# Hybrid decoder step: the second recurrent block's inputs and scan are issued later, the decayed queries earlier, and one small output leaves by another queue

## The chip, the cores and the metric

One core of a Trainium2 chip. The metric is the device time of one execution in microseconds (us). The kernel before takes 1018.92 us, the median of three timed runs (1018.92, 1018.47 and 1023.57).

## The reference

One inference step of a one-layer decoder, on 560 tokens: 16 meta tokens, a prompt of 512, and 8 running sequences of 4 tokens each. All is float32.

```python
def trunk(x, W, states):
    x = x + 0.5 * swiglu(rmsnorm(x, g_ff1), ff1_gate, ff1_up, ff1_down)
    mix, new_st = mixer(rmsnorm(x, g_mix), W, states)
    x = x + mix
    x = x + 0.5 * swiglu(rmsnorm(x, g_ff2), ff2_gate, ff2_up, ff2_down)
    return rmsnorm(x, g_final), new_st
```

`mixer` has two halves that read the same normalised input. The first is a matrix-memory LSTM of four heads of 128: with queries q, keys k, values v and two gates per head it computes, chunk by chunk,

```python
s   = einsum('bhtd,bhsd->bhts', q, k) * w_intra
num = einsum('bhts,bhse->bhte', s, v) + w_inter * einsum('bhed,bhtd->bhte', C0, q)
den = sum(s, -1) + w_inter * einsum('bhd,bhtd->bht', n0, q)
h   = num / maximum(abs(den), exp(-m))
C   = decay * C0 + einsum('bhs,bhse,bhsd->bhed', w_state, v, k)
n   = decay * n0 + einsum('bhs,bhsd->bhd', w_state, k)
```

The second is a linear recurrence over 512 channels, held as four blocks of 128: a causal convolution of width 4 gives xc, two block-diagonal products give the gates r and i, and

```python
a    = exp(-8 * r * softplus(-lambda))
b_in = sqrt(1 - a*a) * (i * xc)
h[t] = a[t] * h[t-1] + b_in[t]
```

The outputs are the 544 rows of y and the new states of both halves.

## The kernel before

Everything is kept transposed: channels lie on the 128 partitions, tokens along the free axis. Each float32 weight tile is split into a high part (whi, cast on ACT, L259) and the rest (wlo, a subtraction on DVE, L264); a product is three matmuls for every tile and half of the tokens: whi by the high part of the input, whi by its low part, wlo by its high part (`split_mm`, L285; the products of the mixer have L296). Weights stream in on SP's queue (L226), six buffers deep. The two feed-forward networks take the time up to about 376 us and from about 645 us on; the mixer lies between.

In the mixer, PE makes 25 products of 1024 by 128: k, q, v, o for heads 0 to 3 and x, y for blocks 0 to 3. A step is one short function, named by a few letters and by its head or block. The table `PLAN` lists all steps in the order in which they are issued, and within `manual_schedule` this order is kept on PE, ACT, DVE and POOL alike, so that each engine works off its own instructions in that order and waits on semaphores for what other engines owe it. SP's DMAs alone are placed by the scheduler. The steps that matter here are these, for head h or block ct:

- `ev` (L1316, code L991) brings the product v from PSUM to the tile vT on DVE, multiplied by the norm's factor; `eq`, `ek`, `ex`, `ey`, `eo` do so for the other products.
- `cx` (L1165) is the convolution on DVE, `hx` (L1174) its split and two small copies on POOL (L1176, L1177), `a` and `b` the gate products on PE (L1191, prg).
- `cj` (L1226) makes the inputs of the recurrence on DVE, three instructions and a small memset (L1229 to L1232); `cd` (L1240) finishes them and runs the scan (L1243, L1244, L1246).
- `s` (L1433) makes the scores in PSUM (pA and pB), `m` (L1452) multiplies them on DVE into the weights W, `sd` (L1461) adds up the parts of W on POOL into D, `hd` (L1333) splits D into zh on ACT and zl on DVE (L1320, L1321).
- `qw` (L1471) makes on POOL the decayed queries qw (L1475) and their products qn with the normaliser state n0 (L1477), 128 by 32 each, and then adds a 32 by 32 piece of W to qn (L1479).
- `n` (L1482) makes numerator and denominator on PE. Its matmuls in order: two of four columns each on qw and the old state c0 (L1489), one on W and the values (L1493), two more on qw, and so on; the denominator takes zh after six of the columns' matmuls and zl near the end (L1497), and qn comes last (L1512). `cn` copies the result away on ACT.
- `cw` (L1565) decays c0 on POOL in eight pieces, `p` (L1554) makes px, what the new tokens add to the state, and `cp` (L1571) adds px to c0 on DVE (L1582) and sends it out.
- `cm` (L1528) splits the squares on ACT (L1531) and DVE (sql, L1532) and takes a maximum (dd, L1534); `f` (L1537) sums the squares on PE (pv, L1541); `cf` (L1544) adds that to dd on DVE (L1548) and takes the root. `vm` (L1378) makes Vm.

Products, scores, gates, n, p, f and the transposes all take turns in three PSUM buffers (tag "mm"); a product may start when the tile that was in its buffer three turns ago has been read. So n of head 1 takes the buffer of product v2, o1 takes that of px of head 2, and n of head 3 takes that of f of head 2. 23 buffers of 128 by 592 (`slot`) hold the tiles of the mixer.

The program's end (L849 to L885) finishes the last three output tiles, the norm, the output y and the last states. There SP and ACT both issue DMAs.

Of the kernel before, what the change touches and what calls it, by code (L numbers as in the profile page):

```python
# [8 lines left out]
ALU = mybir.AluOpType  # L9
# [27 lines left out]
k0 gc  # L37
q0 ek0 gd
k1 eq0 gf ge L0 ex0 cx0 tv0 gp ek1 hq0 hk0 gq hx0 gh
x1 am0 hk1 ex1 cv0  # L40
q1 a0 eq1 w0 b0 ta0 s0 m0 cx1 tk0 tb0 ck0 ca0
v1 sd0 ev1 hq1 L1 hx1 cb0 hd0 qw0 vm0 n0 cw0 a1 cc0 sk0 b1 cd0 cn0 ta1 cm0 tb1
k2 ca1 cb1 ek2 ci1 tv1 am1
x2 f0 cv1 p0 ex2 cf0 tk1 ck1 cp0 cj1 cx2
q2 L2 s1 w1 m1 sd1 eq2 hx2 hq2
v2 ev2 cd1 hd1 a2 ta2 ca2 b2 cb2 vm1 sk1 qw1 tb2 n1 cw1 cc2 cn1 hk2 am2 ce0
x3 cm1 ex3 f1 cf1 ce1
k3 w2 cl1 tv2 cx3
q3 cv2 ek3 hx3 eq3 p1 s2 tk2 cp1 cd2 ck2
v3 qw2 m2 vm2 L3 a3 sd2 hd2 ev3 n2 cw2 ta3 ca3 b3 hk3 cb3 cn2 tv3 tb3 cc3 sk2 am3 cd3  # L50
o0 p2 hq3 cv3 ce2 ce3 eo0 cl2 cl3 cm2 w3 cp2
y0 qw3 to0 ln lr ey0 gy0
o1 eo1 mo0 s3 my0 m3 f2 sd3
y1 tk3 hd3 cf2 to1 ey1 gy1 ck3 so0 mo1 n3 cw3 sk3 cn3 cm3
y2 ey2 so1 f3
# [18 lines left out]
LATER = 3  # L74
# [54 lines left out]
WO = (0, 512, 912, 1184, 1328, 1344)  # L129
# [5 lines left out]
O_HP, O_HS, O_CP, O_CS, O_NP, O_NS = 0, 4, 36, 48, 144, 148  # L135
# [4 lines left out]
def hymba_step(ctx, tc, xT, wgu1, wdn1, win, wout, wgu2, wdn2, consts, small, c0t, wrg,  # L140
               y, o_small, o_m, o_cp, o_cs):
    nc = tc.nc
    act, dve, pool, pe = nc.scalar, nc.vector, nc.gpsimd, nc.tensor
# [175 lines left out]
    osm = cst.tile([P, NOUT], F32, name="osm")  # L319
# [20 lines left out]
    def tmp(name="tmp"):  # L340
        return tp.tile([P, T], F32, tag="t", name=name)
# [8 lines left out]
    class Norm:  # L350
# [38 lines left out]
        def mean(self):  # L389
            self.ps = [aux_tile("psn")[:, :(T - self.c0) // 2] for _ in range(2)]  # L390
            for hf in range(2):
                pe.matmul(self.ps[hf], one_m[1024], self.acc[:, self.half(hf)], start=True, stop=True)
            self.t = tmp("rn")
# [263 lines left out]
    n1 = Norm(G1, 0)  # L657
# [90 lines left out]
    n2 = Norm(G2, C16)  # L748
    n2.open()
    spill = ctx.enter_context(tc.tile_pool(name="spill", bufs=1, space=bass.MemoryType.DRAM))  # L750
    kv = spill.tile([LATER, 2, P, 516], F32, name="kv")
    kv4 = spill.tile([LATER, C16, 257], F32, name="kv4")
    mixer(tc, dict(locals()))


    with tc.tile_pool(name="hp2", bufs=1) as hp, tc.tile_pool(name="sp2", bufs=1) as sp:
# [41 lines left out]
        h = ffn(1, n2, C16, hp, FF2, MID2, dict(ar=out_start, o=out_both, kr=reload, kt=reload4))  # L798
# [5 lines left out]
        def scale(a, b, eng, d0, d1, q):  # L804
            x = X[:, d0:d1, C16 + a:C16 + b]
            eng.tensor_tensor(x, x, rf[:, a:b].unsqueeze(1).to_broadcast([P, d1 - d0, b - a]), op=ALU.mult)
            q.dma_start(y[d0:d1, :, a:b].rearrange("d p t -> p d t"), x)

        def last_mm(hf, d, fs):
            a, b = parts[hf]  # L810
            for f in fs:
                wh, wl = w[d - TAIL][(f - c0) // 4]
                o = (f - c0) % 4 * P
                for m, (u, v) in enumerate(((wh, h[f][0]), (wh, h[f][1]), (wl, h[f][0]))):
                    pe.matmul(pd[d - TAIL][:, hf, :b - a], u[:, o:o + P], v[:, C16 + a:C16 + b],  # L815
                              start=f == c0 and m == 0, stop=f == c1 - 1 and m == 2)
# [3 lines left out]
        def into_x(hf, d):  # L820
            a, b = parts[hf]
            x = X[:, d, C16 + a:C16 + b]
            dve.scalar_tensor_tensor(x, pd[d - TAIL][:, hf, :b - a], 0.5, x, op0=ALU.mult, op1=ALU.add)
            sq[hf, d] = out_square(d, a, b)
# [7 lines left out]
        def root(hf):  # L832
            a, b = parts[hf]
            rsqrt(rf[:, a:b], sq[hf], tmp("rn")[:, :b - a])

        def state(i):
            (k, v), t = keys[i], tails[i]
            py = st[i] = mm_tile("st")[:, 0, :129]
            for j in range(4):
                pe.matmul(py, k[:, P * j:P * j + P], v[:, 129 * j:129 * j + 129], start=j == 0, stop=False)  # L840
            pe.matmul(py, t[:, :P], t[:, P:], start=False, stop=True)

        def state_out(i):
            act.copy(cp[:, i, :], st[i][:, :P])
            act.copy(osm[:, O_NP + i:O_NP + i + 1], st[i][:, P:])
            nc.scalar.dma_start(o_cp[i], cp[:, i, :])

        fs = range(c0, c1)
        with tc.manual_schedule(engines=MANUAL | {mybir.EngineType.Pool}):  # L849
            for d in range(TAIL, KD):  # L850
                last_mm(0, d, fs)
                into_x(0, d)
            a, b = parts[0]
            last_mm(1, TAIL, fs[:2])
            mean(0, 0)
            mean(0, 1)
            last_mm(1, TAIL, fs[2:4])
            mean(0, 2)
            last_mm(1, TAIL, fs[4:])
            root(0)  # L860
            scale(a, b, pool, 3, 4, nc.sync)
            scale(a, b, dve, 0, 3, nc.sync)
            into_x(1, TAIL)
            scale(a, b, dve, 4, 6, nc.sync)
            last_mm(1, TAIL + 1, fs)
            into_x(1, TAIL + 1)
            scale(a, b, dve, 6, 8, nc.sync)
            last_mm(1, TAIL + 2, fs)
            into_x(1, TAIL + 2)
            a, b = parts[1]  # L870
            for i in range(3):
                mean(1, i)
            root(1)
            st = {}
            cp = tmp("cp")[:, :LATER * P].rearrange("p (a b) -> p a b", b=P)
            for i in range(LATER):
                state(i)
            state_out(0)
            scale(a, b, pool, 7, 8, nc.scalar)
            state_out(1)  # L880
            scale(a, b, pool, 6, 7, nc.scalar)
            for d0, d1 in ((0, 1), (1, 3), (3, 5), (5, 6)):
                scale(a, b, dve, d0, d1, nc.sync)
            state_out(2)
            nc.sync.dma_start(o_small[:, O_NP:O_NP + LATER], osm[:, O_NP:O_NP + LATER])  # L885


@with_exitstack
def mixer(ctx, tc, e):
    nc = tc.nc  # L890
    act, dve, pool, pe = nc.scalar, nc.vector, nc.gpsimd, nc.tensor
    C, X, sm, om, osm, one_m = e["C"], e["X"], e["sm"], e["om"], e["osm"], e["one_m"]
    nm, n2 = e["nm"], e["n2"]
# [7 lines left out]
    def slot(name="slot", dtype=F32):  # L901
        return mp.tile([P, 592], dtype, tag="s", name=name, bufs=SLOTS)
# [7 lines left out]
    def blk4(ap):  # L910
        return ap.rearrange("p (b j) -> p b j", j=4)
# [392 lines left out]
    D = [{} for _ in range(H)]  # L1304
# [155 lines left out]
    @step  # L1460
    def do_sd(h):  # L1461
        W = D[h]["W"]
        S = D[h]["S"] = slot("D")
        pool.tensor_copy(S[:, 0:112], W[:, 0:112])
        pool.tensor_tensor(S[:, 112:512], W[:, 112:512], W[:, 512:912], op=ALU.add)
        pool.tensor_tensor(S[:, 240:512], S[:, 240:512], W[:, 912:1184], op=ALU.add)
        pool.tensor_tensor(S[:, 368:512], S[:, 368:512], W[:, 1184:1328], op=ALU.add)
        pool.tensor_tensor(S[:16, 496:512], S[:16, 496:512], W[:16, 1328:1344], op=ALU.add)

    @step  # L1470
    def do_qw(h):  # L1471
        d = D[h]
        qw = d["qw"] = mp.tile([P, NB, 4], F32, tag="qw", name="qw", bufs=2)
        qn = d["qn"] = mp.tile([P, NB, 4], F32, tag="qn", name="qn", bufs=2)
        pool.tensor_tensor(qw, blk4(d["q"][:, 512:TQ]), d["Wb"], op=ALU.mult)  # L1475
        n0 = d["n0"] = C[:, N0 + 8 * h:N0 + 8 * h + 8]
        pool.tensor_tensor(qn, qw, n0.unsqueeze(2).to_broadcast([P, NB, 4]), op=ALU.mult)  # L1477
        qs = qn.rearrange("p b j -> p (b j)")[:32]
        pool.tensor_tensor(qs, qs, d["W"][:32, WO[5]:WO[5] + 32], op=ALU.add)  # L1479

    @step
    def do_n(h):  # L1482
# [243 lines left out]
```

## Time and profile before

| | |
|---|---|
| timed runs | 1018.92, 1018.47, 1023.57 us |
| profiled execution, its own time | 1023.64 us |
| its span, first to last instruction | 1021.9 us |
| mean granted TensorE clock | 0.993 |
| busy: PE, DVE, ACT, POOL | 1013.1, 832.3, 559.5, 127.3 us |
| DMA | 102.85 MB, 101 GB/s |

The times of the rows below are microseconds from the first instruction. In a row of the timeline stand start, duration, engine, source line, operation, output and inputs, the number of instructions that were drawn together, and in brackets how long the engine had been idle and who ended it. In a row of the stage table stand the stretch and its length, then for PE, PE's weight loads, DVE, ACT and POOL the busy time (with the number of instructions), then the granted TensorE clock (1.00 is full speed), the DMA engines' busy share and GB/s.

### The profile page before, as it was taken

How to read it: one execution, taken by the hardware profiler on the slowest of the kernel's cores; microseconds unless marked ns; L12 is line 12 of the kernel's file. 1: busy time of each engine (PE TensorE's matmuls, PEld its weight loads, DVE VectorE, ACT ScalarE, POOL GpSimd, SP SyncE). 2: the span in 40 equal slices, each digit the busy share in tenths (PEclk: the TensorE clock that was granted, in tenths of full speed). 3: DMA queues.
4: the chain of work that ended last, by engine and by line, in shares of the span. 5: the costliest groups of instructions: out<-in, count | busy, mean ns of one | idle time of the engine just before them, and what ended most of it. 6: DMA issues, size and time to landing. Idle time of an engine off the chain costs nothing.

```text
span 1021.9 us, 20228 instructions
## 1 busy us (share of the span) xinstructions
PE 1013.1 (99%) x7778; PEld 997.5 (98%) x7778; DVE 832.3 (81%) x1480; ACT 559.5 (55%) x1074; POOL 127.3 (12%) x187
## 2 busy tenths in 40 slices
PE   9999999999999999999999999999999999999998
PEld 9999999999999999998999999999999999999997
DVE  7988888888788797889678765799888899859774
ACT  6544555565644464576666743554555665654543
POOL 1000000000000044382452202100000000000003
PEclk9999999999999999999799999999999999999999
DMA  6223233223332333325153133223323323335222
GB/s 234 92 79 103 89 100 104 94 95 103 89 104 68 106 116 130 102 81 146 35 133 103 57 104 108 73 64 103 112 87 102 105 94 114 93 102 156 81 70 96
DMA packets 61033, 102.85 MB, mean 101 GB/s; under 512 B 8560, under 2 KB 17024, under 8 KB 60936
## 3 DMA queue, kind: packets, MB, share of 16 engines
q1 hardware_dynamic: 60072, 101.11, 31.6%
q8 instruction: 61, 1.00, 0.4%
q10 hardware_dynamic: 864, 0.45, 0.2%
q14 instruction: 36, 0.29, 0.1%
HBM read 95.20 MB, written 6.33 MB: 99 GB/s over the span
## 4 chain that ended last, share of the span: by engine, by line
PE 88%; DVE 6%; ACT 2%; issue 1%; POOL 1%; DMA 1%; SPq 0%; DVEq 0%; POOLq 0%; ACTq 0%
PE pb L410 26%; PE pad L410 20%; PE pd L296 15%; PE po L296 7%; PE pu L296 4%; PE pg L296 3%; PE px L296 3%; PE pk L296 2%; PE py L296 1%; PE pq L296 1%; PE pn L1493 1%; DVE wlo L264 1%; PE pd L815 1%; PE pv L296 1%; PE pn L1489 1%
## 5 line engine op out<-in xcount | busy, mean ns | idle before, releaser
L259 ACT CAST whi<-raw 128x512 fp32r<-128x512 f32 (+2 forms) x289 | 172.3, 606 | 163.2 <-PE pad L410 41.3
L264 DVE TENSOR_TENSOR wlo<-raw,whi 128x512 fp32r<-128x512 f32 (+2 forms) x289 | 197.6, 700 | 65.5 <-ACT whi L259 62.7
L259 ACT CAST whi<-s 128x512 fp32r<-128x512 f32 x180 | 111.7, 621 | 105.2 <-PE pb L410 37.3
L264 DVE TENSOR_TENSOR wlo<-s,whi 128x512 fp32r<-128x512 f32 x180 | 124.1, 691 | 13.2 <-ACT whi L259 6.8
L410 PE MATMUL pad<-q21h,whi 128*128 128x280 f32 (+1 forms) x360 | 104.2, 290 | 0.1
L410 PE MATMUL pb<-qt4l,whi 128*128 128x280 f32 (+1 forms) x360 | 104.0, 289 | 0.0
L410 PE MATMUL pad<-q21l,whi 128*128 128x280 f32 (+1 forms) x360 | 104.0, 289 | 0.0
L410 PE MATMUL pad<-q21h,wlo 128*128 128x280 f32 (+1 forms) x360 | 104.0, 289 | 0.0
L410 PE MATMUL pb<-qt4h,whi 128*128 128x280 f32 (+1 forms) x360 | 103.9, 289 | 0.0
L410 PE MATMUL pb<-qt4h,wlo 128*128 128x280 f32 (+1 forms) x360 | 103.9, 289 | 0.0
L410 PEld LDWEIGHTS pad<-q21h,whi 128*128 128x128 f32 x360 | 67.8, 188 | 0.4 <-DVE z L429 0.4
L410 PEld LDWEIGHTS pb<-qt4h,whi 128*128 128x128 f32 x360 | 67.9, 189 | 0.0
L410 PEld LDWEIGHTS pb<-qt4h,wlo 128*128 128x128 f32 x360 | 67.8, 188 | 0.0
L410 PEld LDWEIGHTS pad<-q21l,whi 128*128 128x128 f32 x360 | 67.8, 188 | 0.0
L410 PEld LDWEIGHTS pb<-qt4l,whi 128*128 128x128 f32 x360 | 67.8, 188 | 0.0
L410 PEld LDWEIGHTS pad<-q21h,wlo 128*128 128x128 f32 x360 | 67.8, 188 | 0.0
L239 DVE TENSOR_TENSOR s<-raw 128x512 f32<-128x512 f32 x90 | 61.4, 682 | 2.0 <-DMA raw<-in_wdn 2.0
L296 PE MATMUL pd<-hl,whi 128*128 128x280 f32 (+1 forms) x294 | 61.6, 290 | 0.0
L296 PE MATMUL pd<-hh,whi 128*128 128x280 f32 (+1 forms) x294 | 61.4, 290 | 0.0
L296 PE MATMUL pd<-hh,wlo 128*128 128x280 f32 (+1 forms) x294 | 61.2, 289 | 0.0
L379 POOL TENSOR_TENSOR acc<-acc,sq 128x560 f32<-128x560 f32 (+1 forms) x6 | 9.1, 1518 | 405.3 <-ACT sq L378 405.3
L410 PE MATMUL pb<-q11h,whi 128*128 128x280 f32 (+1 forms) x180 | 52.4, 291 | 0.0
(470 smaller groups left out, 3008.0 us busy)
## 6 DMA issues: line engine op xcount, KB each, us to landing
raw<-in_wgu SPq DMA_DIRECT2D x174, 256.0 KB, 2.7
raw<-in_wdn SPq DMA_DIRECT2D x71, 256.0 KB, 2.7
raw<-in_win SPq DMA_DIRECT2D x50, 256.0 KB, 2.9
raw<-in_wout SPq DMA_DIRECT2D x16, 256.0 KB, 2.7
raw<-in_wdn SPq DMA_DIRECT2D x18, 192.0 KB, 2.4
c<-in_c0t SPq DMA_DIRECT2D x4, 512.0 KB, 5.4
out_o_cs<-c SPq DMA_DIRECT2D x4, 512.0 KB, 4.3
X<-in_xT SPq DMA_DIRECT2D x7, 280.0 KB, 5.4
```

The lines of the kernel that those rows point to most:

```text
L239: dve.tensor_tensor(q[k], q[x], q[y], op=op)
L259: act.copy(ready[i][0][:, :src.shape[-1]], src)
L264: dve.tensor_tensor(lo, src, hi, op=ALU.subtract)
L296: state["mm"] = pe.matmul(ps[:, hf, :n], a[:, ws], b[k][:, c0 + hf * n:c0 + hf * n + n], start=first and j == 0 and i == 0, stop=last and ...
L379: (dve if d == KD - 1 else pool).tensor_tensor(self.acc[:, c0:], self.acc[:, c0:], s[:, c0:], op=ALU.add)
L410: pe.matmul(ps, a[:, k * P:k * P + P], b, start=first and k == 0 and i == 0, stop=k == KD // 2 - 1 and i == 2, skip_group_check=not first)
L815: pe.matmul(pd[d - TAIL][:, hf, :b - a], u[:, o:o + P], v[:, C16 + a:C16 + b], start=f == c0 and m == 0, stop=f == c1 - 1 and m == 2)
L1489: pe.matmul(pn[:, 1, 4 * b:4 * b + 4], d["c0"][:, b, :], d["qw"][:, b, :], start=b == 0, stop=False)
L1493: pe.matmul(pn[:, 0, a:512], V[:KROWS[i], i, :P], W[:KROWS[i], WO[i]:WO[i] + 512 - a], start=i == 0, stop=i == 4)
```

## The change

Four things, three of them in the table and one at the end.

1. `cj1` (inputs of block 1's recurrence) leaves its place ahead of `cx2` and now stands, with `cd1` (scan of block 1), behind `ev2` and `hd1`. `hd1` thus comes ahead of both.
2. Each `qw` goes to where its head's `am` (the masked gates) ends, one to two rows up in the table. As its last instruction read W, which is not there yet at that place, that addition goes to the end of `sd`.
3. `cp2` comes ahead of `cm2` and `w3` instead of behind them.
4. The last DMA of the program, three columns of the normaliser states, is issued by ACT instead of SP.

The instructions are the same as before, apart from their places.

```diff
-x1 am0 hk1 ex1 cv0
+x1 am0 qw0 hk1 ex1 cv0
 q1 a0 eq1 w0 b0 ta0 s0 m0 cx1 tk0 tb0 ck0 ca0
-v1 sd0 ev1 hq1 L1 hx1 cb0 hd0 qw0 vm0 n0 cw0 a1 cc0 sk0 b1 cd0 cn0 ta1 cm0 tb1
-k2 ca1 cb1 ek2 ci1 tv1 am1
-x2 f0 cv1 p0 ex2 cf0 tk1 ck1 cp0 cj1 cx2
+v1 sd0 ev1 hq1 L1 hx1 cb0 hd0 vm0 n0 cw0 a1 cc0 sk0 b1 cd0 cn0 ta1 cm0 tb1
+k2 ca1 cb1 ek2 ci1 tv1 am1 qw1
+x2 f0 cv1 p0 ex2 cf0 tk1 ck1 cp0 cx2
 q2 L2 s1 w1 m1 sd1 eq2 hx2 hq2
-v2 ev2 cd1 hd1 a2 ta2 ca2 b2 cb2 vm1 sk1 qw1 tb2 n1 cw1 cc2 cn1 hk2 am2 ce0
+v2 ev2 hd1 cj1 cd1 a2 ta2 ca2 b2 cb2 vm1 sk1 tb2 n1 cw1 cc2 cn1 hk2 am2 qw2 ce0
 x3 cm1 ex3 f1 cf1 ce1
...
-v3 qw2 m2 vm2 L3 a3 sd2 hd2 ev3 n2 cw2 ta3 ca3 b3 hk3 cb3 cn2 tv3 tb3 cc3 sk2 am3 cd3
-o0 p2 hq3 cv3 ce2 ce3 eo0 cl2 cl3 cm2 w3 cp2
-y0 qw3 to0 ln lr ey0 gy0
+v3 m2 vm2 L3 a3 sd2 hd2 ev3 n2 cw2 ta3 ca3 b3 hk3 cb3 cn2 tv3 tb3 cc3 sk2 am3 qw3 cd3
+o0 p2 hq3 cv3 ce2 ce3 eo0 cl2 cl3 cp2 cm2 w3
+y0 to0 ln lr ey0 gy0
...
-            nc.sync.dma_start(o_small[:, O_NP:O_NP + LATER], osm[:, O_NP:O_NP + LATER])
+            nc.scalar.dma_start(o_small[:, O_NP:O_NP + LATER], osm[:, O_NP:O_NP + LATER])
...
     def do_sd(h):
...
+        qs = D[h]["qn"].rearrange("p b j -> p (b j)")[:32]
+        pool.tensor_tensor(qs, qs, W[:32, WO[5]:WO[5] + 32], op=ALU.add)
...
     def do_qw(h):
...
-        qs = qn.rearrange("p b j -> p (b j)")[:32]
-        pool.tensor_tensor(qs, qs, d["W"][:32, WO[5]:WO[5] + 32], op=ALU.add)
```

On DVE, around the evacuation of v2 (vT) and ahead of Vm of head 1, th and a_6071 are the inputs of block 1's recurrence, hs its scan, and zl<-D is the split of head 1:

```order
 L991 TENSOR_TENSOR vT<-pv,r 128x560
+L1321 TENSOR_TENSOR zl<-D,zh 128x512
+L1229 TENSOR_TENSOR th<-th,a_6071 128x584
+L1230 SCALAR_TENSOR_TENSOR th<-th,xc 128x584
+L1231 TENSOR_SCALAR a_6071<-a_6071 128x584
+L1232 MEMSET a_6071 128x8
 L1243 SCALAR_TENSOR_TENSOR th<-th 128x584
 L1244 COPY th<-C 128x8
 L1246 SCALAR_TENSOR_TENSOR hs<-a_6071,th 128x584
-L1321 TENSOR_TENSOR zl<-D,zh 128x512
 L1381 TENSOR_TENSOR Vm<-V5s,seqm 96x1024
```

The four instructions of `cj1` come from ahead of `cx2`, and the split now stands first behind vT; from Vm on the order is as it was.

On POOL, between the sums D of head 1 and the decay of its state c0 (c_5909 and c_5914 are the same tile), osm<-xp are the two copies of `hx2`:

```order
 L1467 TENSOR_TENSOR D<-D,W 128x144
 L1468 TENSOR_TENSOR D<-D,W 16x16
+L1470 TENSOR_TENSOR qn<-qn,W 32x32
 L1176 COPY osm<-xp 128x3
 L1177 COPY osm<-xp 128x24
-L1475 TENSOR_TENSOR qw<-qT,Wb 128x32
-L1477 TENSOR_TENSOR qn<-qw,C 128x32
-L1479 TENSOR_TENSOR qn<-qn,W 32x32
-L1568 TENSOR_SCALAR c_5909<-c_5909,Wb 128x128 x8
+L1568 TENSOR_SCALAR c_5914<-c_5914,Wb 128x128 x8
```

The decayed queries are gone from this place; they now stand ten instructions earlier, behind the masked gates of head 1, and only the addition of W is left.

On DVE, near the end of the product y0, c_6283 is the state of head 2, sql and dd are `cm2`, and rlt belongs to the recurrence's norm:

```order
 L991 TENSOR_TENSOR og<-po,r 128x544
 L1259 TENSOR_TENSOR lacc<-lacc,lsq 128x544 x2
+L1582 TENSOR_TENSOR c_6283<-c_6283,px 128x1024
 L1532 TENSOR_TENSOR sql<-sq,sqh 128x544
 L1534 TENSOR_TENSOR dd<-dd,Eb 128x544
-L1582 TENSOR_TENSOR c_6283<-c_6283,px 128x1024
 L264 TENSOR_TENSOR wlo<-raw,whi 128x512 x2
 L331 SCALAR_TENSOR_TENSOR rlt<-pl,rl 128x544
```

The addition that reads px of head 2 out of its PSUM buffer has moved ahead of two instructions, and what follows is unchanged.

## Prediction

> **What bounds the kernel now.** I read the page's engine row and its clock row first.
>
> ```profile
> PE 1013.1 (99%) x7778; PEld 997.5 (98%) x7778; DVE 832.3 (81%) x1480; ACT 559.5 (55%) x1074; POOL 127.3 (12%) x187
> PEclk9999999999999999999799999999999999999999
> ```
>
> PE is busy for 99% of the span, so only two things can be taken from it: idle time, and time at less than the full clock. The clock row is full but for one of forty slices, at half of the span, inside the mixer. Next come PE's waits, summed, number, longest:
>
> ```profile
> PE pn L1489 <- POOL qn L1477: 1.5, 1, 1.5
> PE po L296 <- DVE c L1582: 0.9, 1, 0.9
> ```
>
> The first is n of head 1, waiting for the decayed queries; the second is o1, waiting for `cp2`. The change moves what ends each of them. Then the table by stages: n of head 0, product x2 with f0, a stretch of DVE, the idle time, n of head 1, x3 with f1, the second idle time, the start of o1, and n of head 3.
>
> ```profile
> 443.68:449.35 5.67, 5.67 (x33) 4.18 (x33) 5.57 (x8) 1.32 (x3) 5.45 (x5) 1.00 0.62 192
> 457.90:464.13 6.23, 6.23 (x51) 6.23 (x50) 5.04 (x11) 4.75 (x10) 1.82 (x6) 1.00 0.40 123
> 470.97:492.99 22.02, 20.51 (x115) 17.09 (x113) 21.49 (x36) 12.49 (x24) 14.52 (x18) 0.81 0.46 134
> 482.20:483.71 1.51, 0.00 (x1) 0.03 (x1) 1.51 (x4) 1.27 (x2) 1.39 (x5) 1.00 0.16 37
> 483.71:493.84 10.13, 10.13 (x33) 7.33 (x34) 8.93 (x14) 5.64 (x6) 10.09 (x10) 0.54 0.21 73
> 493.84:502.24 8.40, 8.40 (x50) 8.40 (x51) 3.40 (x8) 4.63 (x11) 2.31 (x10) 0.74 0.18 62
> 547.30:548.21 0.91, 0.00 (x1) 0.00 (x1) 0.91 (x2) 0.89 (x2) 0.48 (x2) 1.00 0.00 0
> 551.00:555.00 4.00, 4.00 (x31) 3.90 (x31) 3.33 (x6) 2.33 (x5) 0.00 (x0) 1.00 0.39 137
> 564.18:570.13 5.95, 5.95 (x33) 4.45 (x34) 3.73 (x5) 5.27 (x9) 5.46 (x8) 1.00 0.00 1
> ```
>
> Right behind the idle 1.51 us the clock falls: 0.54 over n of head 1, 0.74 over x3. The same 33 matmuls take 10.13 us there and 5.67 at head 0, and x3 with f1 takes 8.40 where x2 with f0 takes 6.23. So the one wait costs 1.51 + 4.46 + 2.17 = 8.14 us. The idle 0.91 us at o1 was followed by no fall (1.00).
>
> The Trainium skill, page "TensorE: Matmul & The Clock Gate", section "Why this matters for your kernels", asks only for no idle gaps above about 3 us. The trace disagrees, with 1.51 us ahead of a half clock; by that rule the wait would cost 1.51 alone.
>
> **The wait at n of head 1.** PE, POOL and DVE around it, and two rows of head 0's time:
>
> ```profile
> 483.71 0.58 PE L1489 MATMUL pn<-qw,c 128*128 128x4 f32 x4 [1.51 <-POOL qn L1477]
> 481.86 0.54 POOL L1468 TENSOR_TENSOR D<-D,W 16x16 f32<-16x16 f32 x1
> 482.36 0.64 POOL L1176 COPY osm<-xp 128x3 f32<-128x3 f32 x1
> 483.11 0.24 POOL L1475 TENSOR_TENSOR qw<-qT,Wb 128x32 f32<-128x32 f32 x1
> 483.43 0.24 POOL L1477 TENSOR_TENSOR qn<-qw,C 128x32 f32<-128x32 f32 x1
> 470.97 0.76 DVE L1229 TENSOR_TENSOR th<-th,a 128x584 f32<-128x584 f32 x1
> 472.83 0.57 DVE L1169 TENSOR_SCALAR xc<-xp,C 128x584 f32<-128x584 f32 x1
> 482.88 0.73 DVE L991 TENSOR_TENSOR vT<-pv,r 128x560 f32<-128x560 f32 x1
> 486.62 1.21 DVE L1381 TENSOR_TENSOR Vm<-V5s,seqm 96x1024 fp32r<-96x1024 f32 x1
> 435.94 0.87 PE pB L1443 x6
> 444.12 0.49 SPq L1342 DMA_DIRECT2D Ab<-rows  x1
> ```
>
> The queries stand on POOL behind the D sums and two copies; moved up, they are done long before. What can still hold PE is vT, since n takes the PSUM buffer of product v2. `cj1` takes DVE from 470.97 to 472.83, 1.86 us. Without it there, the chain of convolution, weight split, scores' product and D sums runs 1.86 us earlier: vT ends at 482.88 + 0.73 - 1.86 = 481.75, ahead of the gate products' end at 482.20, and D at 481.86 + 0.54 - 1.86 = 480.54, so that its split is there before n wants it. I take this wait at nothing, with 0.45 us of cover; if vT were later than that, PE would wait for the excess. With no idle time, the clock should hold: -8.14 us on PE up to the end of x3. One wait is new ahead of this: as the `slot` buffers fall to other tiles, SP's load of head 1's gate rows (Ab) also waits for the scores of head 0 on PE, and later weights queue behind it on SP. It was issued at 444.12 and the scores end at 436.81, so it costs nothing.
>
> **What DVE gives back at f1.** The four instructions go back in behind vT, still ahead of Vm. DVE therefore does the same work before Vm, and Vm starts where it did, at 486.62. The stretch 470.97 to 492.99 above is 21.49 of 22.02 busy: DVE is full there, and the half clock hid it. Behind that stretch stand these rows:
>
> ```profile
> 496.22 0.69 DVE L1321 TENSOR_TENSOR zl<-kT,zh 128x512 fp32r<-128x512 f32 x1 [3.23 <-ACT zh L1320]
> 496.83 1.28 DVE L264 TENSOR_TENSOR wlo<-raw,whi 128x512 fp32r<-128x512 f32 x2
> 500.04 0.73 DVE L1532 TENSOR_TENSOR sql<-sq,sqh 128x544 fp32r<-128x544 f32 x1 [1.93 <-ACT sqh L1531]
> 500.68 0.72 DVE L1534 TENSOR_TENSOR dd<-dd,Eb 128x544 f32<-128x544 f32 x1
> 501.33 0.17 DVE L1158 COPY xp<-C 128x24 f32<-128x24 f32 x1
> 502.20 0.45 DVE L1160 TENSOR_TENSOR xp<-px,r 128x280 f32<-128x280 f32 x1 [0.70 <-PE px L296]
> 502.99 0.71 DVE L1548 TENSOR_TENSOR dd<-pv,dd 128x544 f32<-128x544 f32 x1
> 502.00 0.29 PE L1541 MATMUL pv<-sqh,ones_r 128*128 128x272 f32 x1
> ```
>
> The 3.23 and 1.93 us of idling wait for PE's late n and x3, and go. From 492.99 on, zl (0.61, start to start), two wlo (1.28 less 0.07 of overlap, as at zl) and sql (0.64) end at 495.45. PE's second matmul of f1 needs sql, and would be there at 502.00 - 8.14 + 0.13 (6.23 over 48) = 493.99. So PE waits 1.46 us at f1 and leaves it 6.68 us earlier than before, not 8.14. DVE then needs `cm1`'s maximum (0.65), a small fill (0.17) and the evacuation of x3 (502.99 - 502.20 = 0.79) ahead of L1548, which starts at 497.06 instead of 502.99: the vector chain is 5.93 us earlier. From below, were DVE 1.5 us quicker, f1 would not wait; from above, DVE's idle 0.53 us shows that a little more than 22.02 us is not excluded either. I take 1.46.
>
> **o1 and n of head 3.** Up to o1 PE has no other wait; DVE's rows there and at n of head 3:
>
> ```profile
> 545.67 0.71 DVE L1532 TENSOR_TENSOR sql<-sq,sqh 128x544 fp32r<-128x544 f32 x1
> 546.94 1.21 DVE L1582 TENSOR_TENSOR c<-c,px 128x1024 f32<-128x1024 f32 x1
> 563.41 0.71 DVE L1548 TENSOR_TENSOR dd<-pv,dd 128x544 f32<-128x544 f32 x1
> 563.79 0.27 PE L1356 MATMUL pt<-ident,t 128*96 128x128 f32 x1
> 564.18 0.61 PE L1489 MATMUL pn<-qw,c 128*128 128x4 f32 x4
> ```
>
> `cp2` now takes the place of sql: its addition ends at 545.67 - 5.93 + 1.21 = 540.95, and PE is ready at 547.30 - 6.68 = 540.62. A wait of 0.33 us is left and o1 starts 7.26 us earlier. But sql and dd follow it, so DVE as a whole is no earlier than its 5.93. At n of head 3 PE needs L1548 of `cf2`, which ends at 564.12; PE itself ended its transposes at 564.06, so there is no slack. With the change PE comes at 564.06 - 7.26 = 556.80 and the tile is free at 564.12 - 5.93 = 558.19: a wait of 1.39 us. What `cp2` won at o1 is given back there. n of head 3 starts 5.93 us earlier, and behind it no wait of PE's list is left but the end's.
>
> The other queries moved on POOL (heads 0, 2, 3) pass transposes' inputs and sums that PE takes later, and cost two times 0.24 us in front of them; POOL is 12% busy, and I put them at nothing. The same holds for the small copy of `cp2` on ACT, now ahead of the cast in `cm2`.
>
> **The end.**
>
> ```profile
> 1018.04 0.34 ACTq L846 DMA_DIRECT2D out_o_cp<-cp  x1
> 1018.80 0.46 SPq L885 DMA_DIRECT2D out_o_small<-osm  x1
> SPq L1707 <- DMA out_o_small<-osm: 1.5, 1, 1.5
> ```
>
> The last DMA is issued at 1018.80 behind SP's outputs, and the end waits 1.5 us for it. From ACT it can go behind the issue at 1018.04, at about 1018.40, 0.4 us sooner; then SP's last output, issued just ahead of it, is next. Between 0 and 0.46 us, I take 0.3.
>
> **The sum.** The profiled execution took 1023.64 us, its span 1021.9 and 1.7 around it: 1023.64 - 8.14 (idle and half clock) + 1.46 (f1) - 0.91 + 0.33 (o1) + 1.39 (n of head 3), which is -5.87 and agrees with DVE's 5.93, and - 0.3 at the end: 1017.5. How does that stand to the median? Two of the timed runs took 1018.47 and 1018.92, one 1023.57. The two lie 4.7 to 5.2 us below the profiled one, and a run in which the 1.51 us of idling did not bring the half clock would by this working take 1023.64 - 5.93 = 1017.7, because DVE's full stretch holds it all the same. So I read the median as a run without the half clock. There the change gains only what DVE lets it: the end's 0.3, 1018.4. Between 1017.5 and 1018.4 I forecast **1018.0 us**, no change that can be told: 0.5% or 5.1 us is about what a measurement of this kernel can tell from none.
>
> **Rivals.**
>
> *n of head 3 loses its clock.* Its wait of 1.39 us lies between the 0.91 that did nothing and the 1.51 that brought the half clock, and ahead of the same sparse matmuls. If the clock falls there, 4.46 + 2.17 = 6.63 us are lost and nothing behind recovers them, PE being full to the end: 1018.0 + 6.6 = 1024.6, slower. It decides from an idle time of somewhere between 0.91 and 1.51 us, and in the median only if most runs show it. For it: half of the four executions shown seem to have had it with 1.51. Against: 0.12 us less, and any slip of DVE's 5.93 shortens it. Chance 0.17. The same page of the Trainium skill, section "What's actually happening", has the clock judged in a free-running window of about 3.4 us; by that this would strike some runs and not others, and no run here shows the window.
>
> *DVE is no bound.* If DVE runs through its stretch quicker, PE keeps all: 1023.64 - 8.14 - 0.91 - 0.3 = 1014.3, at most 0.5% below the median. Against it stand 21.49 busy of 22.02. Chance 0.08, and this is the most that the rows allow.
>
> *The wait stays under another name.* If vT comes over 1.5 us later than worked out, PE idles for DVE instead of POOL, the clock falls, and the time is that of the profiled run less the end, 1023.3. Against: DVE's order is free of anything slow there. Chance 0.06.
>
> **The numbers.** My case has 0.69. Range 1015.2 to 1024.2: below, DVE half as much of a bound; above, the third case and most of the first rival. Faster by over 0.5% (below 1013.8) lies beyond even the second rival: 0.04. Slower by over 0.5% (above 1024.0) is most of the first rival: 0.13. Within: 0.83.
>
> **What would show it.** Right: no idle time at n of head 1, granted clock 1.00 from 480 to 505, new waits of PE for DVE's sql at f1 (about 1.5 us) and for L1548 at n of head 3 (about 1.4), o1's wait at about 0.3, and the last DMA issued on ACT near 0.4 us after ACT's last state. Wrong: a clock below 0.9 behind n of head 3, a wait for vT at n of head 1, or neither of the two new waits, which would mean that DVE was not full.

## The result and the profile after

The changed kernel took 1026.82 us (median of 8 executions, 1021.03 to 1027.14), the kernel before 1019.07 (8, 1018.45 to 1023.57). The ratio is 1.0052, interval 1.0031 to 1.0073: slower, where I had forecast 1018.0 and no change that can be told. The medians alone would give 1.0076. Neither median is that of one time: both kernels' executions fall into groups, and the mean granted clock goes with the groups.

| kernel | full clock | in between | lost most |
|---|---|---|---|
| before, 104 executions of all comparisons | 55 at 1018.2 to 1019.9 (clock 0.998 to 1.000) | 21 at 1021.5 to 1022.4 (0.994) | 28 at 1023.1 to 1024.6 (0.992 to 0.993) |
| changed, 19 executions | 4 at 1020.2 to 1021.0 (0.999 to 1.000) | 3 at 1022.0 to 1025.2 (0.993 to 0.998) | 12 at 1026.6 to 1027.2 (0.992 to 0.993) |

(Five executions of all kernels, with a mean clock below 0.9, are left out of these counts and those below.) A mean clock of 0.998 can hide one short stretch at half clock: 3.4 us at half lower the mean over 1020 us by 0.0017, and a profile with 0.998 told below has such a stretch. Of the 55, 11 have 0.998, all from 1019.2 us on; the group is counted as full clock all the same. So two things are to be explained: 1.9 us more at full clock (middle of the groups, 1018.75 and 1020.6), and about 6 us more in most executions.

The profiled execution of the changed kernel is one of the four: 1021.03 us, span 1019.3. Its engine row and its clock row:

```profile
PE 1007.0 (99%) x7778; PEld 991.6 (97%) x7778; DVE 835.3 (82%) x1480; ACT 559.7 (55%) x1074; POOL 129.8 (13%) x187
PEclk9999999999999999999999999999999999999999
```

Its waits of PE (sum, number, longest):

```profile
PE pv L1541 <- DVE sql L1532: 1.6, 1, 1.6
PE pn L1489 <- DVE dd L1548: 1.3, 1, 1.3
PE pt L1356 <- POOL t L1351: 1.2, 2, 0.8
...
PE pA L1443 <- DVE kT L993: 0.8, 1, 0.8
```

The wait for the queries and the half clock behind it are gone, and that for `cp2` at o1 too. The two new waits that were forecast are there with nearly the forecast sizes: 1.57 us at f1 (1.46) and 1.28 at n of head 3 (1.39). Two more were not forecast, for POOL's copy t and for DVE's kT; the one for kT stands in the kernel before as well, in an execution at full clock (0.82 us). The same in the rows of PE's timeline:

```profile
482.27 0.30 PE L1191 MATMUL prg<-xch,wrgl 128*128 128x292 f32 x1
482.41 0.50 PE L1489 MATMUL pn<-qw,c 128*128 128x4 f32 x4
...
494.35 0.29 PE L1541 MATMUL pv<-sqh,ones_r 128*128 128x272 f32 x1
496.21 0.39 PE L1541 MATMUL pv<-sql,ones_r 128*128 128x272 f32 x1 [1.57 <-DVE sql L1532]
...
561.54 0.61 PE L1489 MATMUL pn<-qw,c 128*128 128x4 f32 x4 [1.28 <-DVE dd L1548]
```

A before at full clock was needed to compare with. The profiled execution of the run "before, gap filled" below is one: it has the order of before and lost no clock. In this table stands where PE starts a step, in us behind its first matmul of product v1 in the same execution (timeline rows of the two runs and of four others told below):

| first matmul of | n head 1 | f1 | product k3 | scores head 2 | o1 | n head 3 | gate product, next network |
|---|---|---|---|---|---|---|---|
| before, full clock | 46.49 | 58.52 | 59.08 | 73.88 | 106.01 | 121.98 | 202.75 |
| changed, full clock | 44.76 | 56.70 | 59.04 | 73.88 | 105.60 | 123.89 | 204.66 |
| part 1 alone | 44.81 | 56.77 | 59.07 | 73.89 | 106.07 | 122.05 | 202.76 |
| part 2 alone | 46.43 | 58.48 | 59.09 | 73.90 | 106.49 | 122.45 | 203.23 |
| part 3 alone | 46.47 | 58.48 | 59.04 | 73.87 | 104.72 | 123.32 | 205.70 |
| changed, cp2 and last DMA as before | 44.76 | 56.70 | 59.02 | 73.86 | 106.48 | 122.46 | 203.07 |

PE reaches n of head 1 and f1 1.8 us sooner, waits, and starts k3 at the very place where it did. All that part 1 wins is given back there. At n of head 3 the changed kernel is 1.9 us later, and it keeps that to the end.

Where the 1.9 us come from is seen on ACT. First before, then the changed kernel, at gy0 (the Gelu of block 0):

```profile
549.83 1.28 ACT L1283 ACT_TABLE_LOAD   x1
552.75 0.66 ACT L1283 ACTIVATE yg<-yg 128x544 f32<-128x544 f32 x1 [1.64 <-DVE yg L991]
```

```profile
548.85 1.28 ACT L1283 ACT_TABLE_LOAD   x1 [3.05 <-DVE yg L991]
550.14 0.66 ACT L1283 ACTIVATE yg<-yg 128x544 f32<-128x544 f32 x1
...
550.71 1.65 ACT L259 CAST whi<-raw 128x512 fp32r<-128x512 f32 x3
```

Before, ACT loads the table of Gelu while it waits for yg. In the changed kernel the load stands behind that wait, and 1.28 us come on top of it. The trace shows what changed: at 548.8 us, right ahead of the load, stands a separate semaphore instruction of L1283, and before there is none ahead of that load. So the wait for DVE's yg is no longer carried by the activation but by an instruction of its own, and the load comes behind it. The reason as I read it in the programs, which no trace shows: with `cp2` ahead of `cm2`, the activation on yg must also wait for ACT's own sqh (L1531), and carries that wait instead. Behind it on ACT come weight casts, and behind those on DVE their rests, W, the split of D, and L1548 that n of head 3 waits for.

At the end, the last DMA was issued 0.43 us after ACT's last state, as forecast (0.4), and gave nothing:

```profile
1015.43 0.34 ACTq L846 DMA_DIRECT2D out_o_cp<-cp  x1
1015.86 0.41 ACTq L885 DMA_DIRECT2D out_o_small<-osm  x1
```

```profile
SPq L1707 <- DMA out_o_small<-osm: 2.1, 1, 2.1
```

From the issue of the last state to the end of the span it is 1019.3 - 1015.43 = 3.87 us; before, 1021.9 - 1018.04 = 3.86. From the issue of the small DMA to the end it is now 1019.3 - 1015.86 = 3.44 us instead of 1021.9 - 1018.80 = 3.10, so what the issue won is lost again behind it. The profile puts SP's last wait down to the small DMA. As the end stands equally far behind the last state in both, it may as well be that state's landing that SP waits for; no run here tells the two apart.

### The profile page after: what moved, and what is told of

Same layout as the page of the kernel before. It is cut to its first block, busy times and chain, and to the rows that moved or that the text cites. A ratio compares the mean times of both kernels' runs of the same rounds, so it can differ in the third digit from the quotient of the medians.

```text
span 1019.3 us, 20230 instructions
## 1 busy us (share of the span) xinstructions
PE 1007.0 (99%) x7778; PEld 991.6 (97%) x7778; DVE 835.3 (82%) x1480; ACT 559.7 (55%) x1074; POOL 129.8 (13%) x187
## 4 chain that ended last, share of the span: by engine, by line
PE 86%; DVE 7%; ACT 2%; issue 2%; DMA 1%; POOL 1%; SPq 1%; DVEq 0%; POOLq 0%; ACTq 0%
PE pb L410 27%; PE pad L410 20%; PE pd L296 15%; PE po L296 6%; PE pu L296 4%; PE pg L296 3%; PE px L296 2%; PE pk L296 2%; PE pq L296 1%; DVE wlo L264 1%; PE py L296 1%; PE pd L815 1%; PE pv L296 1%; ACT W L1423 1%; PE pn L1493 1%
## 5 line engine op out<-in xcount | busy, mean ns | idle before, releaser
L767 POOL TENSOR_TENSOR acc<-acc,sq 128x272 f32<-128x272 f32 (+2 forms) x10 | 9.6, 971 | 343.4 <-ACT sq L765 343.2
```

Of the source, the lines that this page charges most:

```text
L767: pool.tensor_tensor(acc[:, a:b], acc[:, a:b], s, op=ALU.add)
```

## The experiments

### Where the clock is lost

Theory A: the idle time ahead of n of head 3 brings a half clock. Theory B: the longer one at f1 does. The changed kernel once more, with no edit:

> The changed kernel once more, to see at which place the granted clock falls in its executions near 1026.8 us. Theory A (n of head 3): the idle 1.3 us ahead of n of head 3 brings the half clock, so a profiled execution near 1026.8 shows the clock at 0.5 behind about 561 us and full between 480 and 505. Theory B (f1): the idle 1.6 us ahead of f1's second matmul brings it, and the clock is at 0.5 behind about 496 us. Both expect a median of 1026.8 and a few executions near 1021.0.

Measured 1026.7 us median, ratio 1.0037 (1.0016 to 1.0059). The profiled execution was again one with a full clock (1020.19), so it could not show the place. Then the two gaps were filled, one each:

```diff
-        pv = ps["f", h] = mm_tile("pv")
+        pv = ps["f", h] = mm_tile("pv"); [pe.matmul(pv[:, 0, :272], ones_r[128], D[h]["sq"][0][:, :272], start=True, stop=True) for _ in range(10 if h == 1 else 0)]
```

> The changed kernel with ten more matmuls of 272 columns on PE ahead of f1 (they repeat f1's first one and are overwritten), so that PE is idle there for about 0.3 us instead of 1.57; the sums are the same, only work is added. Theory B (f1 brings the half clock): nearly all executions near 1021.0, mean clock 0.999. Theory A (n of head 3): median stays at 1026.8, clock 0.992. Both: in an execution with a full clock the time is 1021.0, since PE waits there for DVE anyway.

```diff
-        for i in range(4):
+        for i in [0, 1, 2, 3] * (4 if what == "k" and h == 3 else 1):
```

> The changed kernel with the four transposes of head 3's keys made four times over (the same values into the same place), so that PE is busy for about 1.3 us more ahead of n of head 3, whose wait falls from 1.3 us to below 0.4. Theory A (n of head 3 brings the half clock): nearly all executions near 1021.0, clock 0.999. Theory B (f1): median stays at 1026.8, clock 0.992.

With n of head 3 filled, all 12 executions lie between 1020.1 and 1020.8. With f1 filled, 8 lie at 1020.0 to 1020.6, one at 1021.65 and 3 at 1026.2 to 1026.7. Waits of PE with n of head 3 filled:

```profile
PE pv L1541 <- DVE sql L1532: 1.5, 1, 1.5
...
PE pn L1489 <- DVE dd L1548: 0.6, 1, 0.6
```

So f1's 1.5 us, left as they were, cost no clock in any of 12, and the wait at n of head 3 is needed for the loss: A. That filling f1 also made the loss rarer (3 of 12 at the full loss, against 12 of 19; 4 of 12 against 15 of 19 with the smaller losses) is not explained by A. These numbers do not settle whether it is chance.

Next, the wait at n of head 3 made longer:

```diff
+        [dve.tensor_tensor(nt, dd, dd, op=ALU.add) for _ in range(2 if h == 2 else 0)]
         dve.tensor_tensor(halves(dd, 272), pv[:, :, :272], halves(dd, 272), op=ALU.add)
```

> The changed kernel with two more additions on DVE (128 by 544, 0.72 us each, into a tile that is overwritten) ahead of the one that n of head 3 waits for, so that its idle time is about 2.7 us instead of 1.3. Theory A: every execution shows the half clock there, median 1020.5 + 1.4 + 6.3 = 1028.2, none below 1026. If the chance does not depend on the length of the idle time: a quarter of the executions at 1022.

Median 1028.86 us, all six between 1026.8 and 1030.0 with a clock of 0.991 to 0.993; A holds. Here the profile shows the place, in the row of PE's timeline and in the stages around it (granted clock is the third number from the right):

```profile
562.85 1.02 PE L1489 MATMUL pn<-qw,c 128*128 128x4 f32 x4 [2.87 <-DVE dd L1548]
```

```profile
494.00:500.00 6.00, 4.49 (x35) 4.27 (x34) 4.88 (x10) 1.04 (x1) 5.64 (x17) 1.00 0.26 90
...
560.00:566.00 6.00, 3.15 (x9) 2.12 (x9) 5.04 (x8) 4.29 (x5) 1.98 (x2) 0.73 0.10 36
566.00:572.00 6.00, 6.00 (x21) 4.48 (x20) 3.96 (x7) 2.72 (x6) 5.13 (x6) 0.50 0.00 0
572.00:578.00 6.00, 6.00 (x26) 5.50 (x26) 1.52 (x3) 2.96 (x7) 0.00 (x0) 0.50 0.00 0
578.00:585.00 7.00, 7.00 (x51) 7.00 (x51) 3.33 (x6) 1.79 (x3) 0.00 (x0) 0.87 0.23 77
```

Behind f1's wait (494 to 500) the clock stays at 1.00, behind n of head 3 it is half for 2 x (0.27 x 6 + 0.50 x 6 + 0.50 x 6 + 0.13 x 7) = 17.1 us.

The same on the kernel before, at n of head 1:

```diff
-        for hf in range(2):
+        for hf in [0] * (ct == 2 and g == 1) + [0, 1]:
```

> The kernel before with half of the last gate product ahead of n of head 1 (six matmuls) made twice, the same values into the same place, so that PE idles about 0.7 us there instead of 1.51. Theory A (an idle of 1.3 to 1.5 us ahead of n's sparse matmuls brings the half clock in a part of the executions): no execution near 1021.7 to 1023.8 any more, all between 1018.2 and 1020, median 1018.8, clock 0.998 to 1.000. If the half clock comes from elsewhere: about two in five executions stay above 1021.5.

A miss in size, by my own edit: half of a gate product is three matmuls, not six, so the idle time only fell to 1.16 us. Of 12 executions 8 lay at 1018.4 to 1019.6 and 4 at 1022.0 to 1022.5; the group near 1023.5 was gone. So 1.16 us there seem still too many for the clock to be safe; the place of these four losses was not profiled.

### Which part costs what

Each part alone on the kernel before, as numbered under the change. Part 1:

```diff
-x2 f0 cv1 p0 ex2 cf0 tk1 ck1 cp0 cj1 cx2
+x2 f0 cv1 p0 ex2 cf0 tk1 ck1 cp0 cx2
-v2 ev2 cd1 hd1 a2 ...
+v2 ev2 hd1 cj1 cd1 a2 ...
```

> The kernel before with the first part of the change alone (cj1 and cd1 behind ev2 and hd1). If this part alone takes the wait at n of head 1 away (D and with it the queries come 1.7 us sooner on POOL) and DVE gives all of it back at f1: no idle time at n of head 1, 1.5 us at f1, product k3 at the same place as before, no half clock anywhere, all executions between 1018.3 and 1019.2, median 1018.7. If the queries' move is needed too: the wait at n of head 1 stays above 1 us and a part of the executions stays above 1021.5.

Part 2, all four `qw` as in the change's diff, with the addition of W in `sd`; of the table, the row of head 1's:

```diff
-k2 ca1 cb1 ek2 ci1 tv1 am1
+k2 ca1 cb1 ek2 ci1 tv1 am1 qw1
```

> The kernel before with the second part of the change alone (the decayed queries one stage up). Theory: the wait at n of head 1 stays, 1.2 to 1.5 us, but for DVE's vT instead of POOL's queries, and so does the half clock in a part of the executions: groups near 1019 and 1022 to 1024 as before. If POOL was the only cause of that wait: no idle time there, all executions below 1019.5.

Part 3:

```diff
-o0 p2 hq3 cv3 ce2 ce3 eo0 cl2 cl3 cm2 w3 cp2
+o0 p2 hq3 cv3 ce2 ce3 eo0 cl2 cl3 cp2 cm2 w3
```

> The kernel before with the third part of the change alone (cp2 ahead of cm2 and w3). Theory: this part alone puts the load of the Gelu table behind the wait for yg, n of head 3 starts 1.8 us later, with an idle time of about 1.3 us ahead of it. Without any half clock 1020.4, with one at n of head 3 1026.7, with one at n of head 1 about 1024.5; median above 1023, slower than before by 0.3% or more. If the cost needs the other parts: as before, groups at 1018.7 and 1022 to 1024.

Part 1: median 1018.76 us, all 12 between 1018.2 and 1019.6, ratio 0.9971 (0.9957 to 0.9986). It takes the wait at n of head 1 away by itself, and with it the lost clock; at full clock it moves nothing behind f1 (table above). Part 2: 1021.01 us, ratio 0.9996 (0.9976 to 1.0015), six executions at 1018.8 to 1019.8 and six at 1022.2 to 1024.8. The wait of PE at n of head 1 stays and only changes its name:

```profile
PE pn L1489 <- DVE vT L991: 1.5, 1, 1.5
...
PE pt L1356 <- POOL t L1351: 0.8, 1, 0.8
PE po L296 <- DVE c L1582: 0.6, 1, 0.6
```

It also brings the 0.8 us for POOL's t ahead of the transposes of v3, and o1 is 0.48 us later. Part 3: 1026.5 us, ratio 1.0057 (1.0029 to 1.0084), five executions above 1030, which fits a loss at both n, though none of these five was profiled. Its profiled execution, the waits at both n and the stages behind them:

```profile
PE pn L1489 <- POOL qn L1477: 1.5, 1, 1.5
PE pn L1489 <- DVE dd L1548: 1.5, 1, 1.5
```

```profile
487.00:494.00 7.00, 7.00 (x49) 6.28 (x49) 6.74 (x13) 6.81 (x14) 7.00 (x6) 1.00 0.10 39
...
560.00:566.00 6.00, 4.96 (x19) 3.36 (x19) 4.66 (x7) 5.28 (x6) 3.40 (x5) 0.72 0.08 30
566.00:572.00 6.00, 6.00 (x44) 5.32 (x43) 3.21 (x7) 4.78 (x13) 1.96 (x4) 1.00 0.00 0
```

The same 1.5 us left the clock alone at n of head 1 (1.00) and took 2 x 0.28 x 6 = 3.4 us at half from n of head 3, where the rows say 0.72. It starts o1 1.29 us sooner and n of head 3 1.34 later. (Its 205.70 at the end of the table includes what the half clock behind n of head 3 took.) The parts add up: 202.75 + 0.48 (part 2) + 1.34 (part 3) = 204.57, and the changed kernel has 204.66. Part 4, the last DMA, has no run of its own; this sum leaves nothing for it.

Two ways back, both on the changed kernel. Part 3 undone, and the last DMA on SP again:

```diff
-o0 p2 hq3 cv3 ce2 ce3 eo0 cl2 cl3 cp2 cm2 w3
+o0 p2 hq3 cv3 ce2 ce3 eo0 cl2 cl3 cm2 w3 cp2
...
-            nc.scalar.dma_start(o_small[:, O_NP:O_NP + LATER], osm[:, O_NP:O_NP + LATER])
+            nc.sync.dma_start(o_small[:, O_NP:O_NP + LATER], osm[:, O_NP:O_NP + LATER])
```

> The changed kernel without two of its parts: cp2 back behind cm2 and w3, and the last DMA back on SP. The program then loads the Gelu table ahead of the wait for yg, as before. Theory A with the late table load caused by cp2's new place: DVE's chain behind gy0 is 1.3 us earlier, o1 waits about 0.9 us for cp2 again, n of head 3 waits less than 0.4, no half clock there, time about 1019.8 in nearly all executions. Theory B (f1 alone decides): most executions still above 1024.

Median 1019.03 us, all 12 between 1018.8 and 1019.7, ratio 0.9980 (0.9967 to 0.9992). The 1.5 us at f1 are there in it and cost no clock: B is out. And the table alone:

```diff
         act.activation(rv, pl, AF.Abs_reciprocal_sqrt, bias=eps_c)
+        act.activation(mp.tile([P, 1], F32, name="g1", bufs=1), eps_c, AF.Gelu_apprx_tanh)
```

> The changed kernel with one more Gelu activation of 128 by 1 on ACT, ahead of gy0, so that the 1.28 us load of its table no longer stands behind the wait for yg. Theory A, with the late table load as the cause of DVE's lateness there: gy0 and all behind it on ACT and DVE come 1.2 us sooner, the wait at n of head 3 falls from 1.30 us to below 0.3, the executions with a full clock take 1019.8 us, and nearly all have a full clock. Theory B: 1019.8 with a full clock, but most executions still lose their 5.8 us at f1, median about 1025.6. If the table load costs nothing: 1026.8 as before.

n of head 3 starts 1.32 us sooner (122.57 in the terms of the table), and executions at full clock take 1018.9 to 1019.5 us. The wait there fell less than expected, from 1.3 to 1.1 us, because PE came sooner too (two short waits ahead of it went). So the clock is not safe: 3 of 11 executions took 1023.7 to 1023.8. The late table load costs what was expected; the idle time that it was to remove stayed. So most of the wait at n of head 3 is not the load's doing: PE has no wait at o1 any more, but L1548 starts no sooner for it (121.80 us behind v1's first matmul; 121.68 with `cp2` in its old place, in the run just told), and PE waits 1.08 us for it even without the late load.

### DVE and POOL side by side

In the changed kernel L1548 came later than I had worked out. Rows of DVE and POOL there:

```profile
495.21 0.94 DVE L1532 TENSOR_TENSOR sql<-sq,sqh 128x544 fp32r<-128x544 f32 x1
496.07 1.55 DVE L1534 TENSOR_TENSOR dd<-dd,Eb 128x544 f32<-128x544 f32 x1
498.42 0.71 DVE L1548 TENSOR_TENSOR dd<-pv,dd 128x544 f32<-128x544 f32 x1
```

```profile
482.80 12.19 POOL L1568 TENSOR_SCALAR c<-c,Wb 128x128 f32<-128x128 f32 x8 [0.86 <-PE pn L1489]
494.95 0.61 POOL L1410 TENSOR_TENSOR Am<-Ab,cmask 128x112 f32<-128x112 f32 x1
495.53 1.51 POOL L1411 TENSOR_TENSOR Am<-Ab,cmask 128x384 f32<-128x384 f32 x1
```

In the row that I had used, the maximum (L1534) took 0.72 us. Two trials moved POOL's work. In the first, on the changed kernel, am2 comes ahead of cw1 on POOL:

```diff
-v2 ev2 hd1 cj1 cd1 a2 ta2 ca2 b2 cb2 vm1 sk1 tb2 n1 cw1 cc2 cn1 hk2 am2 qw2 ce0
-x3 cm1 ex3 f1 cf1 ce1
+v2 ev2 hd1 cj1 cd1 a2 ta2 ca2 b2 cb2 vm1 sk1 tb2 n1 cc2 cn1 hk2 am2 qw2 ce0
+x3 cm1 ex3 f1 cf1 cw1 ce1
```

> The changed kernel with cw1 (POOL's eight decays of head 1's state) behind head 2's masked gates on POOL, so that POOL's 128 by 384 addition no longer runs beside DVE's sql and maximum ahead of f1's end. If DVE and POOL slow each other there (1.55 us for the maximum instead of 0.72): sql and the maximum take 0.72 each, f1's wait falls from 1.5 to about 1.2, L1548 comes 0.8 us earlier and PE's waits for kT and V (1.0 us in sum) fall by that; with a full clock 1019.6 to 1020.1 instead of 1020.5. If they don't: no change, 1020.5.

sql and the maximum fell to 0.71 and 0.80 us, and the waits for kT and V went. But am2 now ran beside the scaling of K (0.91 and 1.05 us instead of 0.68 and 0.30), sql was later, and PE waited 2.13 us at f1. Behind that wait the clock fell too (0.72 over 494 to 500; the same once more over 560 to 566, behind 1.3 us of waiting at n of head 3), and the executions at full clock took 1020.0 to 1020.9 as before: the slowing had moved. The second, on the kernel before with part 1:

```diff
-... n1 cw1 cc2 cn1 hk2 am2 ce0
-x3 cm1 ex3 f1 cf1 ce1
+... n1 cw1 cc2 cn1 hk2 ce0
+x3 cm1 ex3 hz3 am2 f1 cf1 ce1
```

where hz3 is the two small copies of `hx3`, which wait for the evacuation of x3.

> The kernel before with the first part of the change, and am2 (POOL's masked gates of head 2) held back until x3 is evacuated, so that its 128 by 384 addition runs beside DVE's wait for ACT instead of beside sql and the maximum of cm1. If POOL slows DVE there: sql falls from 0.95 to 0.72 and the maximum from 1.55 to 0.72 us, L1548 comes 1.0 us sooner, PE's waits for kT and V at the scores of head 2 (1.0 us) go, and with them up to 1.0 us of the time: 1017.7 to 1018.2, full clock in all executions, ahead of the kernel before and of the changed one. If the slowing moves to other instructions: 1018.7 as with the first part alone.

```profile
494.42 0.71 DVE L1532 TENSOR_TENSOR sql<-sq,sqh 128x544 fp32r<-128x544 f32 x1
495.06 0.71 DVE L1534 TENSOR_TENSOR dd<-dd,Eb 128x544 f32<-128x544 f32 x1
...
496.56 0.71 DVE L1548 TENSOR_TENSOR dd<-pv,dd 128x544 f32<-128x544 f32 x1
```

```profile
497.28 1.02 POOL L1411 TENSOR_TENSOR Am<-Ab,cmask 128x384 f32<-128x384 f32 x1
```

Median 1017.3 us, 10 executions from 1016.4 to 1017.7, ratio to before 0.9965 (0.9948 to 0.9982); part 1 alone, in the same comparison, took 1018.76. Both instructions are quick again, POOL's too (1.02 instead of 1.51). Scores of head 2 start 1.02 us sooner than with part 1 alone; at o1 it is 1.36 us, because the wait there falls from 0.91 to 0.56, and by the next network 1.58; the last 0.2 were not traced. This version is ahead of both kernels.

## Why the prediction was wrong, step by step

- **The wait at n of head 1 goes, and the clock holds there.** Right: no idle time, clock 1.00. Part 1 alone does it, through D on POOL.
- **DVE gives it back at f1.** Right: 1.57 us for 1.46, and k3 starts where it did at full clock. That the faster executions of before had no half clock and the change could win nothing against them was right too. I put such an execution at 1017.7 us; they are at 1018.75. The missing 1.0 us is the next point.
- **"The vector chain is 5.93 us earlier."** Mis-sized: 502.99 - 498.42, and 0.41 more because v1 started that much later (its first matmul at 437.65 for 437.24), makes 4.98. I took 0.72 and 0.73 us for the maximum and sql from an execution whose half clock kept POOL's am2 away from them. At full clock they run side by side, in the kernel before as well (its maximum takes 1.53 in the gap-filled run), and the 1.0 us come back as waits for kT and V.
- **The other queries on POOL "at nothing".** Wrong: part 2 alone makes o1 0.48 us later, by the wait for POOL's t.
- **o1 and n of head 3.** o1's wait went altogether (0.33 forecast). The wait at n of head 3 came out at 1.28 for 1.39, for the reason given in the main: with the table loaded early it is still 1.08, because DVE cannot follow what `cp2` wins for PE at o1. That 1.28 lies so near 1.39 is luck in part, since the table load made DVE later and short waits made PE later too. What failed at full clock is the sentence behind it: I followed who waits for whom on PE and DVE, and put the small copy of `cp2` on ACT "at nothing". The move took a wait from one instruction to another, brought the table load behind yg onto the path, and cost 1.34 us.
- **The end, 0.3.** Nothing: 3.87 us for 3.86.
- **The first rival came true, and this is the larger part of the miss.** From the 1018.75 of before, part 2's 0.48 and the table's 1.34 lead to 1020.6; the other 6.2 us up to 1026.8 are the half clock. So the step that failed is the choice to let n of head 3 wait 1.39 us and keep its clock. I had seen that these 1.39 us might bring the half clock, priced it at 6.63 us (6.2 measured), and gave it 0.17, mainly because 1.39 is less than 1.51. It happened at full size in 12 of 19. The chance was argued from too few executions: two numbers, 0.91 and 1.51, at two places, were taken for a threshold. Had it stood near one half, with the table's 1.34, the range would have had to reach 1026 (1018.0 + 1.34 + 6.63).

## What to carry to other kernels

Where a kernel's executions fall into groups, work from a profile of each group: a half clock hides which engines are full and which run side by side. A wait that has vanished is only worth what the next engine in line can follow, and here DVE could not. After moving a step, look also at what its neighbours on ACT now wait for: a table load that stood in the shade of a wait can come out behind it. And a gap of PE ahead of sparse matmuls can be worth more than its length: here gaps of 1.1 to 2.9 us cost several us more, in some executions or in all.

## What the runs showed of the hardware

The chance that the clock is lost depends on the place and the length of PE's idle time:

| idle ahead of | length, us | executions with a lost clock (with those at 0.998) |
|---|---|---|
| n of head 3, filled (its matmuls have 4 columns among others) | 0.6 | 0 of 12 |
| n of head 3, table early; n of head 1, gap filled | 1.1 to 1.2 | 7 of 23 |
| n of head 1, before | 1.5 | 49 of 104 (60) |
| n of head 1, part 2 alone | 1.5 | 6 of 12 (7) |
| n of head 3, changed | 1.3 | 14 of 19 (15) |
| n of head 3, f1 filled | 1.3 | 3 of 12 (4) |
| both n, part 3 alone | 1.5 | 9 of 12 (12) |
| n of head 3, made longer | 2.9 | 6 of 6 |
| f1, between two full products | 1.3 to 1.5 | 0 of 46 (3) |
| f1, and n of head 3 with 1.3 (cw1 late) | 2.1 | 9 of 12, the profiled one at both places |

The place of a loss is seen in four profiles only; in the other rows it follows from the experiments. That 1.3 us at n of head 3 would strike more often than 1.5 at n of head 1 cannot be read from this: with those at 0.998 it is 19 of 31 against 67 of 116.

The stretches at half clock that the profiles show are 3.4, 13.7 (before, by the two rows of the prediction's stage table: 2 x (0.46 x 10.13 + 0.26 x 8.40)) and 17.1 us long, that is 1, 4 and 5 times 3.4. The Trainium skill, page "TensorE: Matmul & The Clock Gate", section "What's actually happening", states a free-running window of about 3.4 us; these lengths agree. Whether it runs freely no run here shows, and what makes a loss last one such length, four or five stays open.

The other is that DVE and POOL slow each other: POOL's addition of 128 by 384 took 1.51 instead of 1.02 us, and DVE's maximum of 128 by 544 took 1.55 instead of 0.71, when they ran side by side. Not every pair does so equally: beside POOL's eight decays (482.80 to 494.99) the changed kernel's two additions L1229 took 0.75 and 0.82 us.
